# A two-layer hybrid decoder trunk: another order for its opening, and other rules for the list that orders its engines

## The chip, the cores and the metric

The kernel runs on one core of a Trainium2 chip, as one launch. The metric is the device time of that launch in microseconds (us). Before the change the median of three runs is 1262.36 us (1260.78 to 1263.79). The profile used here is of one further execution, which took 1262.23 us. Its profiled span, from the first to the last instruction, is 1260.5 us, so 1.73 us lie around the span.

## The reference

The program is a trunk of two layers over 256 tokens of width 1024, all in float32. Cut to what matters:

```python
c_act = silu(c)
for l in range(2):
    mod = c_act @ w_ada[l] + b_ada[l]                 # 1024 x 6144
    sh1, sc1, g1, sh2, sc2, g2 = split(mod, 6)
    h = rms_norm(x, norm1_g[l]) * (1 + sc1) + sh1
    proj = h @ w_in[l]                                # q k v iq ik iw z xbc dt ga gm
    q, k = rope(rms_norm(q)), rope(rms_norm(k)); iq, ik = rope(iq), rope(ik)
    # per block of 128 queries: score by iq, ik, iw; keep 64 keys; softmax attention on them
    o_attn = dsa_attention(q, k, v, iq, ik, iw, 64) @ w_attn_o[l]
    y = ssd_scan(silu(conv4(xbc)), softplus(dt), A)   # Mamba-2, then gate by silu(z), group norm
    mixed = (sigmoid(ga) * o_attn + sigmoid(gm) * (y @ w_ssm_o[l])) @ w_out[l]
    x = x + g1 * mixed
    h = rms_norm(x, norm2_g[l]) * (1 + sc2) + sh2
    val, gate = split(conv3(h @ w_up[l]), 2)
    x = x + g2 * ((silu(gate) * val) @ w_down[l])
```

## The kernel before

**The products.** Every weight matrix is streamed from HBM in units of up to 4 x 128 rows by 512 columns (1 MB). ACT rounds a unit to its high part `wh` (fp32r), DVE takes the low part `wl` = `st` - `wh`. The activations `h` are kept in the same two parts. A product is then three matmuls on PE: high by high, low weight by high, high weight by low activation. PE is busy with these almost throughout; the other engines prepare weights and evaluate what lies between products.

**The engines' order.** The program writes no order for ACT, DVE, POOL and the loads. Each operation is entered in a list with an estimate of its duration and its dependences. `plan_ahead` (line 122) plays the list forward: for each engine it takes the entered operation that could start first, where an operand that another engine or a transfer makes counts as there some time (`HOP`, line 59) after its end. `commit` issues all that the plan starts before PE's own clock `now` (line 190, where every row of the profile therefore says L190). PE's instructions are placed at once, in the order in which the code reaches them; `on_pe` (line 386) keeps the modelled time, and doubles the price of matmuls for a while after a long modelled wait. `pump` lets waiting tasks (attention, scan, transposes) put their matmuls in between as soon as the model says that their operands are there. So a number in `HOP` or in the price of a load changes no computation, but the order on all five engines, to the end of the program.

**The loads.** All weights come over SP's one DMA queue, at most six units ahead. Weight units have three buffers (`wst`), the modulation's units five (`wop`).

**The opening** (`run_open`, line 764). The first layer's norm needs shift and scale, 2048 columns of the modulation, which are 8 MB of `w_ada` in 8 units. They are done in four quarters `q` of 2 x 256 columns. In each quarter PE multiplies two units (`ada_products`: 16 matmuls of 32x128 from `st`, twice, into one bank), ACT copies the result (`adarow`), PE turns it, DVE makes `mod` and `amul`, and `norm_tile` makes two of the eight tiles of `h`, their high part on ACT and the low one on DVE. With two tiles of `h` the products with two of the eight row blocks of the first K columns, of the index queries IQ and of a narrow block (`misc`: index key, weights, dt) can be done. These are the `fills`: per quarter four, two for K with misc (9 matmuls each) and two for IQ (6 each). A fill is given to PE while the next modulation product is not there by the plan (line 839), or ahead of the next quarter's weights. The tables for the rotation (cosine, sine; `tables`, line 1003) are entered in quarter 1. `warm_up(n)` issues n 128x128 matmuls of ones whose result nobody reads; before the change there are 10 ahead of quarter 0 and 8 behind it.

In names: `st` is a loaded unit, `wh`, `wl` its parts, `w_4` the replicated silu(c), `rows` the small vectors before they are turned into `vec`, `bk` a PSUM bank, `p` the index scores, `top` the eight largest of them, `mx` the softmax maximum, `sp_p` the polynomial for softplus.

Of the kernel before, what the change touches and what calls it, by code (L numbers as in the profile page):

```python
# [46 lines left out]
def trunk(ctx, tc, x, c, positions, w_ada, b_ada, norm1_g, w_in, q_norm_g, k_norm_g, ssm_conv_w, ssm_conv_b,  # L47
# [6 lines left out]
    now = [0.0]  # L54
# [1 line left out]
    URGENT = 200  # L56


    HOP = dict(dve=33.0, act=33.0, pool=79.0, pe=54.0, dma=2500.0, dma_act=0.0, dma_pool=0.0)
    LAP = dict(dve=75.0, act=100.0, pool=30.0, dma=0.0, dma_act=0.0, dma_pool=0.0)  # L60
    CROWD = 0.18
    ORDER = ("dve", "act", "pool", "dma", "dma_act", "dma_pool")
    free_at = dict.fromkeys(ORDER, 0.0)
    waiting = {k: [] for k in ORDER}
# [57 lines left out]
    def plan_ahead():  # L122

        if not stale[0]:
            return
        stale[0] = False
        at = dict(free_at)
        todo = {k: list(v) for k, v in waiting.items() if v}
        crowd, slow = crowd_done[0], None
        for v in todo.values():  # L130
            for w in v:
                w.end = None
        while todo:
            best = None
            for key, ws in todo.items():
                first = None
                for w in ws[:1] if key == "dma" else ws:
                    t = w.least
                    for d in w.deps:
                        e = d.end  # L140
                        if e is None:
                            t = None
                            break
                        e += (HOP[key] if d.key[:3] != "dma" else HOP["dma"]) if d.key != key else -LAP["act"] if key == "act" else 0.0
                        if e > t:
                            t = e
                    if t is None:
                        continue
                    t = max(t, at[key])
                    if first is None or t < first[0]:  # L150
                        first = (t, w)
                        if t <= at[key]:
                            break
                if first and (best is None or first[0] < best[0]):
                    best = first + (key,)
            t, w, key = best
            w.start, w.end = t, t + w.ns
            if key == "pool":
                w.end = crowded(t, w.ns, crowd)
                slow = w  # L160
            elif w.heavy:
                crowd = w.end
                if slow and slow.end > t:
                    slow.end = crowded(t, slow.end - t, crowd)
                    at["pool"] = max(at["pool"], slow.end - LAP["pool"])
            at[key] = max(t + 0.4 * w.ns, w.end - LAP[key])
            todo[key].remove(w)
            if not todo[key]:
                del todo[key]
# [53 lines left out]
    def hold(tile):  # L223

        held.add(tile.tensor.name)
        return tile
# [130 lines left out]
    def enter_loads():  # L357
        while loads:
            out, src, issue = loads[0]
            t = out.tensor  # L360
            if t.name not in states and getattr(t, "tag", None):
                mine = rings.get(t.tag, ())
                if len(mine) >= (t.bufs or t.tag_meta.bufs) and not ripe(mine[0]):
                    return
            loads.pop(0)
            if not any(o.tensor.name == t.name for o, _, _ in loads):
                on_the_way.discard(t.name)
            give("dma", [out], [src], out.partition_size() * out.free_size() * 4 / (200.0 if now[0] < 1.0 else 300.0), issue, now[0] - 30000.0)

    def after(prev, cur):  # L370

# [14 lines left out]
    def on_pe(o, lhsT, rhs, issue, turn=False):  # L386
# [3 lines left out]
        at = now[0]  # L390
# [4 lines left out]
        ready = at  # L395
        for d in deps:
            if d.key != "pe":
                ready = max(ready, end_of(d, "pe"))
        if ready > at + 3000.0:
            slow_until[0] = ready + 3400.0  # L400
        at = ready
        w = Work("pe", 0.0, (), 0.0, issue)
# [361 lines left out]
    def run_open(ch):  # L764


        misc = hold(bank())
        tm = [[bank(pj) for _ in range(2)] for _ in range(2)]
        fills = []

# [30 lines left out]
        def fill():  # L801
            weigh(*fills.pop(0))

        def modulations():
            for q in range(4):
                ps = bank()
# [11 lines left out]
                        pass  # L818
                fence.clear()
                if q == 1:  # L820
                    for _ in tables():
                        pass
                    ch["start"]()
                while fills and fills[0][0] < q - 1:
                    fill()
                ahead(ch["w"][q], ch["w"][q] + 1)
                if q == 0:
                    ahead(ch["m"], ch["m"] + 1)
                    spare["bank"] = bank()
                    warm_up(8)  # L830
                fills.extend((q, w, j) for w in (1, 0) for j in range(2))

        ahead(0)
        for g in first:
            for _ in g:
                pass
        warm_up(10)
        for need in modulations():
            while fills and fill_need(*fills[0]).at() < need.at() and now[0] < need.at() - FILL:
                fill()  # L840
        ahead(ch["ada"][3][-1])
        done(crep)
        opening_done()
        while fills:
            fill()
        ch["evac"][0](tm[0])

    FILL = 300.0

    def opening_done():  # L850
        commit(1e12)
# [97 lines left out]

    def enter():  # L950
        sums = w_tile("xsum", [P, 2, 2], F32, 1)
        junk = spare["bank"] = bank(pj)
        for t, m4, xs_ in xin:
            A.activation(junk, xs_, AF.Square, accum_out=sums[:, t, m4:m4 + 1])
            ps = bank()
# [847 lines left out]
```

## Time and profile before

| | |
|---|---|
| median of 3 runs | 1262.36 us |
| profiled execution: its time, its span | 1262.23 us, 1260.5 us |
| PE, PEld, DVE, ACT, POOL busy | 97%, 90%, 76%, 60%, 33% |
| granted TensorE clock, mean | 0.989 |
| HBM | 243.89 MB read, 194 GB/s over the span |

The profile's page has busy shares, the span in 40 slices, the chain of waits that ended last, and groups of instructions. Since all instructions have one line, groups are told apart by the names of their tiles. A row of the timeline gives the start, the time until the last of the merged instructions ended, the engine, what it writes and reads, how many, and in brackets how long the engine stood idle before and what ended that. One float32 matmul appears as two records of 128x128, so 8 matmuls of ones are x16.

### The profile page before, as it was taken

The page shows a single profiled execution, that of the slowest core. Times are in us where ns is not written, and L with a number is a line of the kernel's source. Part 1 is how long each engine was busy: PE and PEld are TensorE (multiplying, and loading weights), DVE is VectorE, ACT ScalarE, POOL GpSimd, SP SyncE. Part 2 cuts the span into 40 slices and gives each one's busy share as a digit, 9 for nine tenths or more (in the row PEclk, how much of TensorE's full clock was granted, in tenths as well). Part 3 has the DMA queues.
Part 4 walks back from the last instruction along what each step waited for, and adds up shares of the span by engine and source line. Part 5 has one row for each costly group of instructions (what it writes and reads, how often), then busy time and mean ns, then how long its engine had stood idle before and what let it go on. Part 6 is the DMA issues. An engine that isn't in the chain of part 4 may idle for free.

```text
span 1260.5 us, 24567 instructions
## 1 busy us (share of the span) xinstructions
PE 1225.6 (97%) x9789; PEld 1140.5 (90%) x9789; DVE 956.3 (76%) x1477; ACT 762.2 (60%) x1362; POOL 414.3 (33%) x479
## 2 busy tenths in 40 slices
PE   7789999999999999999999999999999999999998
PEld 6577789999989999999997778999999999999998
DVE  4499977878786778889757997888777766678753
ACT  3356677774764357777436467877467544777742
POOL 2042533343262124564211443323304511335400
PEclk8889999999999999999989999999999999999999
DMA  9654644457456647876756455355764665566542
GB/s 300 231 182 144 209 146 171 163 193 255 159 203 215 234 156 239 276 248 229 247 180 201 148 195 193 126 170 172 240 204 153 215 236 166 181 209 202 195 162 73
DMA packets 158663, 246.53 MB, mean 196 GB/s; under 512 B 11868, under 2 KB 66870, under 8 KB 158549
## 3 DMA queue, kind: packets, MB, share of 16 engines
q1 hardware_dynamic: 157989, 244.77, 58.4%
q8 instruction: 77, 1.26, 0.4%
q14 instruction: 37, 0.30, 0.1%
q0 software_dynamic: 288, 0.19, 0.1%
q10 hardware_dynamic: 272, 0.00, 0.0%
HBM read 243.89 MB, written 1.05 MB: 194 GB/s over the span
## 4 chain that ended last, share of the span: by engine, by line
PE 79%; DVE 12%; ACT 4%; issue 3%; POOL 2%; DVEq 0%; POOLq 0%; ACTq 0%
PE bk L190 79%; DVE wl L190 4%; DVE w L190 1%; ACT wh L190 1%; DVE adacc L190 1%; DVE t L190 1%; DVE p L190 1%; POOL w L190 1%; ACT w L190 1%; ACT p L190 1%; DVE mx L190 1%; DVE ss L190 1%; DVE top L190 0%; POOL rows L190 0%; POOL rr L190 0%
## 5 line engine op out<-in xcount | busy, mean ns | idle before, releaser
L190 PE MATMUL bk<-h,wh 128*128 128x256 f32 x3488 | 646.8, 286 | 0.4 <-ACT h L190 0.4
L190 PEld LDWEIGHTS bk<-h,wh 128*128 128x128 f32 x3488 | 543.4, 192 | 12.1 <-issue 9.6
L190 DVE TENSOR_TENSOR wl<-st,wh 128x2048 fp32r<-128x2048 f32 (+1 forms) x200 | 435.0, 2179 | 146.4 <-ACT wh L190 146.0
L190 PE MATMUL bk<-h,wl 128*128 128x256 f32 x1744 | 492.0, 283 | 0.0
L190 ACT ACTIVATE wh<-st 128x2048 fp32r<-128x2048 f32 (+1 forms) x200 | 352.1, 1768 | 213.2 <-PE bk L190 176.7
L190 POOL TENSOR_TENSOR w<-w,w 128x254 f32<-128x254 f32 (+2 forms) x213 | 208.0, 992 | 416.1 <-DVE w L190 330.2
L190 PEld LDWEIGHTS bk<-h,wl 128*128 128x128 f32 x1744 | 334.1, 192 | 0.5
L190 PE MATMUL bk<-u,wh 128*128 128x256 f32 x1344 | 234.7, 279 | 0.0
L190 PEld LDWEIGHTS bk<-u,wh 128*128 128x128 f32 x1344 | 203.3, 188 | 1.6 <-issue 1.6
L190 PE MATMUL bk<-u,wl 128*128 128x256 f32 x672 | 186.1, 277 | 0.0
L190 PE MATMUL bk<-wh,h 128*128 128x512 f32 x448 | 150.4, 411 | 11.9 <-ACT wh L190 5.2
L190 ACT ACTIVATE w<-bk,vec 128x256 f32<-128x256 f32 (+2 forms) x272 | 122.2, 516 | 33.3 <-DVE w L190 19.6
L190 PEld LDWEIGHTS bk<-u,wl 128*128 128x128 f32 x672 | 126.2, 188 | 0.0
L190 DVE SCALAR_TENSOR_TENSOR adacc<-ad,chalf,adacc 128x512 f32<-128x512 f32 x140 | 121.6, 869 | 4.6 <-DMA ad<-in_w_ada_dram 4.0
L190 PEld LDWEIGHTS bk<-wh,h 128*128 128x128 f32 x448 | 83.8, 193 | 33.6 <-issue 8.0
L190 DVE SCALAR_TENSOR_TENSOR w<-bk,vec,w 128x255 f32<-128x255 f32 (+1 forms) x184 | 81.5, 475 | 16.4 <-ACT w L190 15.8
L190 PE MATMUL bk<-wl,h 128*128 128x512 f32 x224 | 90.4, 404 | 3.3 <-DVE wl L190 3.3
L190 POOL TENSOR_TENSOR u<-u,u 128x256 f32<-128x256 f32 (+1 forms) x56 | 67.3, 1219 | 57.4 <-ACT u L190 33.6
L190 POOL TENSOR_TENSOR rr<-ss,mhalf 128x16 f32<-128x16 f32 x8 | 26.0, 3254 | 98.3 <-DVE ss L190 98.3
L190 PEld LDWEIGHTS bk<-wl,h 128*128 128x128 f32 x224 | 43.4, 194 | 14.1 <-DVE wl L190 5.3
L190 ACT ACTIVATE w<-w 128x256 f32<-128x256 f32 x92 | 35.6, 412 | 30.3 <-POOL w L190 30.1
L190 ACT ACTIVATE u<-bk 128x128 f32<-128x128 f32 (+2 forms) x128 | 32.1, 325 | 30.7 <-PE bk L190 30.6
(194 smaller groups left out, 1178.5 us busy)
## 6 DMA issues: line engine op xcount, KB each, us to landing
st<-in_w_in_dram SPq DMA_DIRECT2D x80, 1024.0 KB, 5.1
st<-in_w_up_dram SPq DMA_DIRECT2D x88, 512.0 KB, 5.4
ad<-in_w_ada_dram SPq DMA_DIRECT2D x160, 256.0 KB, 5.4
st<-in_w_down_dram SPq DMA_DIRECT2D x20, 1024.0 KB, 5.3
st<-in_w_ssm_o_dram SPq DMA_DIRECT2D x16, 1024.0 KB, 5.3
st<-in_w_ada_dram SPq DMA_DIRECT2D x16, 512.0 KB, 10.2
st<-in_w_attn_o_dram SPq DMA_DIRECT2D x8, 1024.0 KB, 5.0
st<-in_w_out_dram SPq DMA_DIRECT2D x8, 1024.0 KB, 5.2
```

What stands on the lines that cost most here:

```text
L190: begun[n].issue()
```

## The change

It has these parts.

1. **The list.** An operand that a transfer brings counts as there 1300 ns after the end of the transfer (2500 before). The transfer itself is priced at 250 bytes per ns before PE's first matmul and 330 after (200 and 300), and starts at 2000 ns at the earliest. PE's price doubles after a modelled wait of 2000 ns (3000). And `PATIENCE`: an operation takes the place of an older one on an engine only if it could start earlier than that by more than 0.35 of its own duration; before, any lead was enough.
2. **The unread products.** They have a PSUM bank of their own from the start of `run_open` (held until the last modulation product), where they shared a bank with the unread result of ACT's squares. `keep_warm(need)` issues as many as fit, by the plan, before the operand that PE would wait for: int((wait - 300 ns) / 225 ns), if more than one. The two fixed lots (10 and 8) go.
3. **Which comes first.** A fill is still given only while the next modulation product is not there by the plan, but its margin `FILL` goes from 300 to 700 ns; with the transfers priced lower, the plan sees a modulation unit there earlier, and its product stands ahead of more fills.
4. **The tables** are entered in quarter 0, not in quarter 1.

```diff
-    HOP = dict(dve=33.0, act=33.0, pool=79.0, pe=54.0, dma=2500.0, dma_act=0.0, dma_pool=0.0)
+    HOP = dict(dve=33.0, act=33.0, pool=79.0, pe=54.0, dma=1300.0, dma_act=0.0, dma_pool=0.0)
+    PATIENCE = 0.35
...
-                    if first is None or t < first[0]:
+                    if first is None or t + PATIENCE * w.ns < first[0]:
                         first = (t, w)
...
-            give("dma", [out], [src], out.partition_size() * out.free_size() * 4 / (200.0 if now[0] < 1.0 else 300.0), issue, now[0] - 30000.0)
+            give("dma", [out], [src], out.partition_size() * out.free_size() * 4 / (250.0 if now[0] < 1.0 else 330.0), issue, max(2000.0, now[0] - 30000.0))
...
-        if ready > at + 3000.0:
+        if ready > at + 2000.0:
             slow_until[0] = ready + 3400.0
...
         misc = hold(bank())
+        spare["bank"] = hold(bank())
...
+        def keep_warm(need):
+
+            n = int((need.at() - now[0] - 300.0) / 225.0)
+            if n > 1:
+                warm_up(n)
...
                 if q == 1:
-                    for _ in tables():
-                        pass
                     ch["start"]()
...
                     ahead(ch["m"], ch["m"] + 1)
-                    spare["bank"] = bank()
-                    warm_up(8)
+                if q == 0:
+                    for _ in tables():
+                        pass
...
-        warm_up(10)
         for need in modulations():
             while fills and fill_need(*fills[0]).at() < need.at() and now[0] < need.at() - FILL:
+                keep_warm(fill_need(*fills[0]))
                 fill()
+            keep_warm(need)
         ahead(ch["ada"][3][-1])
-        done(crep)
+        done(crep, spare["bank"])
...
-    FILL = 300.0
+    FILL = 700.0
...
-        junk = spare["bank"] = bank(pj)
+        junk = bank(pj)
```

What this does to the order is seen at three places. The first is PE at the start of the opening, from behind the turning of the input to the first fill (`bk<-wh,h`); before:

```order
L190 MATMUL bk_137<-ones 128x128 x10
L190 MATMUL bk_143<-st_128,w_4_86 32x128 x16
L190 MATMUL bk_143<-st_129,w_4_86 32x128 x16
L190 MATMUL bk_289<-ident,rr_33_288 128x128 x2
L190 MATMUL bk_291<-ident,rows_81 128x128
L190 MATMUL bk_292<-ident,adarow_285 128x128
L190 MATMUL bk_303<-ones 128x128 x8
L190 MATMUL bk_126<-wh_134,h_294 128x512
```

The same place after the change:

```order
L191 MATMUL bk_124<-ones 128x128 x9
L191 MATMUL bk_144<-st_129,w_4_86 32x128 x16
L191 MATMUL bk_124<-ones 128x128 x11
L191 MATMUL bk_144<-st_130,w_4_86 32x128 x16
L191 MATMUL bk_291<-ident,rr_34_290 128x128 x2
L191 MATMUL bk_293<-ident,rows_81 128x128
L191 MATMUL bk_294<-ident,adarow_287 128x128
L191 MATMUL bk_124<-ones 128x128 x23
L191 MATMUL bk_127<-wh_135,h_296 128x512
```

The unread products stand now before each of the two modulation products, and 23 instead of 8 before the first fill. Two more lots stand behind quarters 0 and 1 (12 and 9).

The second place is PE at the end of quarter 2, where the last modulation unit is multiplied (`st_435` before, `st_481` after) and its result turned (`adarow`); the fills here are those of quarter 2 (K into bk_126 and bk_127 before, IQ into bk_124 and bk_125; one number higher after). Before:

```order
L190 MATMUL bk_125<-wh_564,h_558 128x512
L190 MATMUL bk_125<-wl_565,h_558 128x512
L190 MATMUL bk_125<-wh_564,h_559 128x512
L190 MATMUL bk_124<-wh_564,h_561 128x512
L190 MATMUL bk_124<-wl_565,h_561 128x512
L190 MATMUL bk_124<-wh_564,h_562 128x512
L190 MATMUL bk_125<-wh_564,h_561 128x512
L190 MATMUL bk_125<-wl_565,h_561 128x512
L190 MATMUL bk_125<-wh_564,h_562 128x512
L190 MATMUL bk_566<-st_435,w_4_86 32x128 x16
L190 MATMUL bk_680<-ident,adarow_679 128x128
L190 MATMUL bk_126<-wh_688,h_682 128x512
```

After:

```order
L191 MATMUL bk_123<-h_598,wh_303 128x256
L191 MATMUL bk_602<-st_481,w_4_86 32x128 x16
L191 MATMUL bk_125<-wh_600,h_594 128x512
L191 MATMUL bk_125<-wl_601,h_594 128x512
L191 MATMUL bk_125<-wh_600,h_595 128x512
L191 MATMUL bk_126<-wh_600,h_594 128x512
L191 MATMUL bk_126<-wl_601,h_594 128x512
L191 MATMUL bk_126<-wh_600,h_595 128x512
L191 MATMUL bk_719<-ident,adarow_705 128x128
L191 MATMUL bk_125<-wh_600,h_597 128x512
L191 MATMUL bk_125<-wl_601,h_597 128x512
L191 MATMUL bk_125<-wh_600,h_598 128x512
```

The last modulation product moved ahead of both IQ fills of quarter 2 (12 matmuls), of which now six lie between it and the turning of its result, and six behind that. In quarter 1 the second product and the turning moved in the same way.

The third place is DVE in the first layer's choice of 64 keys, where the two query blocks (128x128 and 128x256) go through eight rounds of eight largest (`MAX`) and their removal (`MATCH_REPLACE`). Before:

```order
L190 SCALAR_TENSOR_TENSOR p_173_1049<-p_198_1143,iws_829,p_173_1049 128x256
L190 MAX top_1168<-p_173_1049 128x8 x2
L190 MATCH_REPLACE p_173_1049<-top_1168,p_173_1049 128x128
L190 MATCH_REPLACE p_173_1049<-top_1168,p_173_1049 128x256
L190 MAX top_1168<-p_173_1049 128x8 x2
```

After:

```order
L191 SCALAR_TENSOR_TENSOR p_173_1095<-p_198_1191,iws_871,p_173_1095 128x256
L191 MAX top_1213<-p_173_1095 128x8
L191 MATCH_REPLACE p_173_1095<-top_1213,p_173_1095 128x128
L191 MAX top_1213<-p_173_1095 128x8
L191 MATCH_REPLACE p_173_1095<-top_1213,p_173_1095 128x256
```

Each removal stands now right behind the search whose result it reads, where the other block's work stood between them. Counted over the whole program, the DVE instructions that read what the one just before them wrote go from 62 to 180 (of 1445): 32 of the 118 more are removals, 29 are on `mx`, 29 on the convolutions' `w`, 15 on the softplus `sp`.

## Rows read from the trace of the kernel before

**Rows 1.** The page: its span, and the chain that ended last by engine.

```profile
span 1260.5 us, 24567 instructions
...
PE 79%; DVE 12%; ACT 4%; issue 3%; POOL 2%; DVEq 0%; POOLq 0%; ACTq 0%
```

**Rows 2.** Windows: stretch, length, busy us of the five engines, clock, DMA share, GB/s.

```profile
20.00:30.00 10.00, 8.86 (x60) 6.95 (x61) 5.08 (x21) 1.62 (x4) 0.00 (x0) 0.83 1.07 360
30.00:40.00 10.00, 4.91 (x45) 3.30 (x44) 6.15 (x25) 5.13 (x12) 0.00 (x0) 0.78 1.06 348
40.00:50.00 10.00, 8.96 (x91) 6.73 (x90) 2.41 (x8) 2.83 (x7) 2.85 (x12) 0.88 0.93 324
...
90.00:140.00 50.00, 48.66 (x250) 37.89 (x249) 48.27 (x117) 29.05 (x62) 15.69 (x14) 1.00 0.45 150
...
200.00:1260.00 1060.00, 1048.64 (x8561) 996.20 (x8560) 804.36 (x1121) 651.36 (x1113) 347.90 (x361) 1.00 0.59 195
```

**Rows 3.** Timeline of PE, last quarter of the opening: start, us, instructions, idle before.

```profile
58.13 1.08 PE L190 MATMUL bk<-st,w 128*32 128x128 f32 x32
...
62.00 0.50 PE L190 MATMUL bk<-wh,h 128*128 128x512 f32 x1 [2.06 <-ACT h L190]
63.06 0.79 PE L190 MATMUL bk<-wl,h 128*128 128x512 f32 x1 [0.56 <-DVE wl L190]
...
70.38 0.84 PE L190 MATMUL bk<-wh,h 128*128 128x512 f32 x3
```

**Rows 4.** Timeline of SP: the issue of the last modulation unit's loads.

```profile
38.41 1.87 SPq L190 DMA_DIRECT2D st<-in_w_ada_dram  x2
```

**Rows 5.** The page's DMA issues: count, KB each, median us to landing.

```profile
st<-in_w_ada_dram SPq DMA_DIRECT2D x16, 512.0 KB, 10.2
```

**Rows 6.** Timeline of PE, starts of the quarters, and the unread products.

```profile
10.41 3.56 PE L190 MATMUL bk<-ones 128*128 128x128 f32 x20 [2.05 <-ACT bk L190]
...
17.08 1.95 PE L190 MATMUL bk<-ones 128*128 128x128 f32 x16
...
21.64 0.62 PE L190 MATMUL bk<-wl,h 128*128 128x512 f32 x1 [1.03 <-DVE wl L190]
...
36.87 0.80 PE L190 MATMUL bk<-wh,h 128*128 128x512 f32 x1 [4.09 <-ACT wh L190]
```

**Rows 7.** Timeline of PE in quarter 1, at full clock.

```profile
42.82 0.50 PE L190 MATMUL bk<-wh,h 128*128 128x512 f32 x1
...
44.75 1.08 PE L190 MATMUL bk<-st,w 128*32 128x128 f32 x32
45.76 0.50 PE L190 MATMUL bk<-wh,h 128*128 128x512 f32 x1
...
47.28 0.27 PE L190 MATMUL bk<-ident,adarow 128*128 128x128 f32 x1
```

**Rows 8.** Timeline of DVE and of ACT (one row), the last quarter's chain.

```profile
59.98 0.23 DVE L190 TENSOR_TENSOR mod<-bk,vec 128x2 f32<-128x2 f32 x2 [8.10 <-PE bk L190]
...
60.93 0.87 DVE L190 SCALAR_TENSOR_TENSOR w<-xt,amul,w 128x256 f32<-128x256 f32 x2
61.72 1.28 DVE L190 TENSOR_TENSOR wl<-st,wh 128x512 fp32r<-128x512 f32 x2
...
61.44 0.91 ACT L190 ACTIVATE h<-w,mod 128x256 fp32r<-128x256 f32 x2 [0.33 <-DVE w L190]
```

**Rows 9.** Timeline of PE behind the opening: the wait for an IQ bank.

```profile
85.46 0.70 PE L190 MATMUL bk<-wh,h 128*128 128x512 f32 x2 [3.58 <-DVE sp_p L190]
```

**Rows 10.** Timeline of DVE: softplus steps one behind the other, then between other work.

```profile
93.10 0.22 DVE L190 TENSOR_TENSOR sp_p<-sp_p,sp_s 128x64 f32<-128x64 f32 x1
93.36 0.19 DVE L190 TENSOR_SCALAR sp_p<-sp_p 128x64 f32<-128x64 f32 x1
...
93.86 0.19 DVE L190 TENSOR_SCALAR sp_p<-sp_p 128x64 f32<-128x64 f32 x1
93.96 0.22 DVE L190 TENSOR_TENSOR t<-bk,sint 128x64 f32<-128x64 f32 x1
```

## The prediction

> **What bounds the kernel now.** I read the page's chain first: PE holds 79% of it and DVE 12% [rows 1]. Then the windows, to see where PE is not full. From 200 us to the end PE is busy for 1048.64 of 1060 us at a clock of 1.00, so 11.4 us are idle there in all; from 90 to 140 us it is busy for 48.66 of 50 while DVE is for 48.27; between 20 and 50 us it is busy for 8.86, 4.91 and 8.96 of 10 us at a clock of 0.78 to 0.88 [rows 2]. The program is bound by PE, and what can be taken is mostly in the opening. There the DMA share is about 1 until 50 us [rows 2], so loads bound the first half; not the second. The loads of the last modulation unit are issued from 38.41 on, the second at 40.28 at the latest [rows 4]; with the median of 10.2 us to landing [rows 5] they are there by 50.5. PE multiplies that unit at 58.13, after all fills of quarter 2, and only then starts the chain to the last two tiles of `h`: the fills of quarter 3 wait until 62.00 and 63.06 [rows 3]. That is 8 us lost by order alone.
>
> **The change part by part.** All is summed against the profiled execution (1262.23 us, against a median of 1262.36, so the same). Prices at full clock: a 9-matmul fill 44.75 - 42.82 = 1.93, a modulation unit 45.76 - 44.75 = 1.01, a 6-matmul fill 47.28 - 45.76 = 1.52 [rows 7], an unread product some 0.23 (8 in 1.95, the last outlasting its step) [rows 6]. The chain of a quarter, from T, when `adarow` is turned: `mod` 0.1 behind, then `amul`, the two `w` from T + 0.55 (before 0.95, with one `wl` of 0.6 between) to T + 1.4, the high `h` 0.5 behind the first `w`, the two low `h` as long as the `w`, to T + 2.35, and `wl` pieces at 0.61 each, of which the third lets the fill's second matmul go: T + 4.2 [rows 8].
>
> Start: loads are issued in the same order up to the 72nd row of SP, the first quarter's weights land when they did, and the low part that freed PE at 21.64 [rows 6] is no earlier. The bank of its own lets the unread products start at about 9 instead of 10.41 [rows 6], since they wait for a DVE copy and not for ACT. The 23 of them take 5.3 us and fit into the wait from some 16.2 to 21.6. So quarter 0 starts at 21.6 as before, but warm: the clock of 0.83 in 20 to 30 us [rows 2] becomes 1.
>
> Quarter 0 from 21.6: fill 23.5, unit 24.5, fill 26.5, fill 28.0, unit 29.0, turning of the small rows and of `adarow` 29.9, fill 31.4, 12 unread products 34.2. Loads bring a unit of 1 MB in 3 us (348 to 360 GB/s [rows 2]), so the two units of quarter 1 should be there at some 23.5 and 26.5. Its chain has one more copy (0.55 us for `vec`), so T = 30.4 and its third `wl` is at 34.6. Quarter 1 starts at 34.6, where before it started at 36.87 after 4.09 us idle [rows 6] and at half clock.
>
> Quarter 1 from 34.6: fill 36.5, unit 37.5, fill 39.5, unit 40.5, fill 42.0, turned 42.3, fill 43.8, 9 unread 45.9, unit of quarter 3 46.9. Its third `wl` (one piece is done early) is at 42.3 + 3.6 = 45.9, so PE does not wait. Quarter 2 from 46.9: fills 48.8 and 50.8, the last unit 51.8 (there by 50.5), fill 53.3, turned 53.6, fill 55.1. Quarter 3: its third `wl` at 53.6 + 4.2 = 57.8, PE having 2.5 us without work between 55.1 and then.
>
> Before, PE needed from 63.06 to 70.6 [rows 3] (the second of the three matmuls there is the first of the next slab) for the rest of quarter 3, 7.5 us, of which I estimate 3.4 at half clock after waits of 2.06 and 0.56 (a clock of 0.83 over 10 us, as behind the wait ahead of quarter 0 [rows 2], is 3.4 us at half). With 2.5 us of waiting again I take the same 7.5: the opening's products end at 57.8 + 7.5 = 65.3 instead of 70.6, a gain of 5.3. If the clock stays up, 1.7 more (half of 3.4): 7.0. If the first fill starts at 22.6, 1 less.
>
> Tables: some 25 small DVE operations, four sines and one ACT table load move from between 23 and 35 us, where they stood ahead of quarter 1's chain, to 11 to 16 us, where DVE and ACT wait for the first units. Their cover is that wait; without it they would cost their 2 to 3 us at the first quarter, which still had the loads of 20 us ahead. I take nothing. The other bank that is held leaves two rotating banks for the opening's small results instead of three; each is read within 0.6 us of being written, so nothing, up to 0.5 us a quarter.
>
> Behind the opening, PE stands 3.58 us at 85.46 [rows 9]: its next slab needs the bank that DVE reads for the rotation of IQ. DVE's work from the K result to that read is the same set of operations, and starts when K's products end, so it moves up with them and the wait stays. From 90 us on PE is bound, and the gain of 5.3 goes through to the end.
>
> The list's numbers: they move some 290 rows of PE and many of DVE, ACT and POOL, all the way to the end, and SP's loads by a few places from the 73rd row on. No matmul comes or goes but 46 unread ones in waits. What this does to the 11.4 us of idle PE behind 200 us cannot be read off: bounds are -4 (a third of it goes) and, from the DVE pairs, +10 (below); I take 0, nearest to the 1% that PE idles there.
>
> The 118 more DVE instructions right behind the one whose result they read: a dependent step starts 93.36 - 93.10 = 0.26 after the one ahead, an independent one 93.96 - 93.86 = 0.10 [rows 10]. So up to 0.16, say 0.13 each, 15 us of DVE. DVE is busy for 804 of 1060 us behind 200 [rows 2], so most of it is free; from 90 to 140, with 48.27 of 50, it is not. [...]
>
> **Rivals.**
> *DVE becomes the bound (slower).* Place: the two dense stretches (90 to 140 us, and its like in the second layer) and the attention between. There are 26 pairs in each of the two (16 removals, about 7 of `sp`, 3 of `ss`) and 29 of `mx`, in all 81; at 0.13 that is 10.5 us. If PE waits for all of it, 1262.23 - 5.3 + 10.5 = 1267.4. It decides from 60 pairs on PE's path on (5.3 + 2.5 = 7.8 us). For it: DVE's 48.27 of 50. Against: the plan sees these pairs and places PE's work later accordingly, and PE waited only 1.34 us in that stretch.
> *The gain is given back (no change).* The opening is 5 us shorter, but the wait of 3.58 us grows, or transfers counted as there 1.2 us earlier than before let ACT and DVE stand in front of one that has not landed. At 3 to 5 us of new waits in 1190 us: 1260 to 1262. For it: small moves in every stage; against: nothing in the opening's sum depends on them.
> *The clock stays up and the list saves too (more).* 7.0 and 3 of the 11.4 us: 1252.2.
> *The order does not move.* Excluded by the order itself, which has the last unit ahead of 12 matmuls.
>
> **How the numbers follow.** Forecast: opening 5.3 us shorter, the rest as it was: 1262.23 - 5.3 = 1256.9, from 1254 to 1259.5 by the clock, the start and 1.5 us of small waits; chance 0.57. More: 0.13. Given back, within 0.2% (2.5 us either way, about what a measurement of this kernel tells from no change): 0.18. Slower: 0.12. So faster 0.70, same 0.18, slower 0.12. The range of 8 in 10 goes from 1251.5 (the third rival) to 1263 (the second with its worst end and a little of the first).
>
> **What would show it.** The last unit's product (`st,w`) at about 51 instead of 58.13; quarter 3's second matmul near 57.8; the first matmul of the next slab near 65.3; a clock of 1 between 20 and 50 us; the 3.58 us still there, some 5 us earlier. Behind 90 us the same idle PE as before within 2 us. I am wrong if the slab behind the opening starts later than 68, if PE's idle time behind 90 us grows by more than 3 us with DVE named as releaser, or if a unit is multiplied late with a DMA named as the releaser.

## The result, and the profile after

The changed kernel is slower: 1279.39 us (1278.67 to 1282.12), against 1262.9 for the kernel before beside it; ratio 1.0137, 95% interval [1.0117, 1.0157]. The forecast was 1256.9. The opening did what was forecast; 22 us are lost behind it.

The page after, span and chain, answers [rows 1]:

```profile
span 1277.3 us, 24697 instructions
...
PE 60%; DVE 20%; ACT 7%; POOL 5%; issue 5%; DMA 2%; SPq 0%; DVEq 0%; POOLq 0%; ACTq 0%
```

PE held 79% of the chain before and 60% now; DVE 20% instead of 12%. More of what the end depends on now runs through engines other than PE.

The windows after, columns as in [rows 2]; the last runs from the first slab behind the opening to the end:

```profile
20.00:30.00 10.00, 10.00 (x95) 8.95 (x94) 5.30 (x11) 3.56 (x8) 0.00 (x0) 1.00 1.06 359
30.00:40.00 10.00, 9.79 (x112) 7.89 (x111) 5.03 (x12) 3.26 (x7) 0.00 (x0) 1.00 1.02 336
40.00:50.00 10.00, 10.00 (x109) 8.30 (x109) 5.08 (x11) 3.33 (x7) 4.97 (x12) 1.00 0.90 311
...
90.00:140.00 50.00, 47.22 (x236) 35.88 (x235) 47.48 (x97) 26.70 (x52) 18.63 (x10) 1.00 0.47 158
...
65.25:1277.30 1212.05, 1179.89 (x9350) 1101.69 (x9348) 943.78 (x1373) 737.33 (x1300) 424.85 (x416) 1.00 0.56 188
```

The stretch of before that answers to the last row:

```profile
70.38:1260.50 1190.12, 1172.71 (x9350) 1099.32 (x9348) 923.92 (x1375) 735.09 (x1302) 403.29 (x416) 1.00 0.58 192
```

The opening runs at a clock of 1.00, where [rows 2] have 0.78 to 0.88. Behind it the same 9350 PE instructions take 1212.05 instead of 1190.12 us, at the same clock of 1.00: 21.9 more. PE's idle time grows from 17.4 to 32.2 us, and PE's recorded busy time by 7.2 us, for the same instructions. At full clock the record of a 128x512 matmul is 0.39 to 0.5 us long, while nine in a row take 1.93 us, 0.21 each; so a wait shorter than the difference shows as busy and not as idle. DVE is busy for 19.9 us more with two instructions fewer.

PE's timeline after, columns as in [rows 3]:

```profile
19.11 5.30 PE L191 MATMUL bk<-ones 128*128 128x128 f32 x46
24.16 0.48 PE L191 MATMUL bk<-wh,h 128*128 128x512 f32 x1
...
36.07 0.48 PE L191 MATMUL bk<-wh,h 128*128 128x512 f32 x1
...
52.27 1.08 PE L191 MATMUL bk<-st,w 128*32 128x128 f32 x32
...
57.57 0.51 PE L191 MATMUL bk<-wh,h 128*128 128x512 f32 x1 [1.10 <-ACT wh L191]
59.38 0.49 PE L191 MATMUL bk<-wl,h 128*128 128x512 f32 x1 [1.30 <-DVE wl L191]
...
65.25 0.84 PE L191 MATMUL bk<-wh,h 128*128 128x512 f32 x3
...
81.11 0.70 PE L191 MATMUL bk<-wh,h 128*128 128x512 f32 x2 [3.79 <-DVE sp_p L191]
```

The last modulation unit is multiplied at 52.27 (before 58.13) and the next slab begins with the second matmul of the row at 65.25, at 65.48 (before 70.60): 5.1 us earlier, where 5.3 were forecast. The wait for the IQ bank is there still, 3.79 for 3.58 [rows 9].

What PE waited for after: us in total, times, the longest.

```profile
PE bk L191 <- DVE wl L191: 5.7, 8, 1.3
PE bk L191 <- DVE t L191: 4.4, 4, 1.7
PE bk L191 <- DVE sp_p L191: 3.8, 1, 3.8
PE bk L191 <- ACT adarow L191: 3.6, 3, 1.6
PE bk L191 <- DVE u L191: 3.2, 5, 1.2
PE bk L191 <- DVE adacc L191: 2.8, 3, 1.5
```

No single wait carries the loss (that for `sp_p` was there before): it is many, none over 1.7 us, most of them for the ends of DVE's chains (`t` the rotation, `u` attention, `adacc` the second layer's modulation, `wl` the weights).

What DVE waited for, two lines of after, then the two of before:

```profile
DVE adacc L191 <- DMA ad<-in_w_ada_dram: 22.5, 17, 3.7
DVE u L191 <- ACT u L191: 22.3, 27, 2.0
```

```profile
DVE u L190 <- ACT u L190: 4.2, 5, 1.4
DVE adacc L190 <- DMA ad<-in_w_ada_dram: 4.0, 1, 4.0
```

So there are two suspects: the loads' numbers (DVE stands 18.5 us longer in front of transfers that have not landed) and the patience (it stands 18 us longer for ACT's `u`); the pairs, DVE instructions right behind the one whose result they read, are a third, and part of the second. These rows are no price by themselves: DVE's longest wait in total, that of `wl` for ACT's `wh`, fell at the same time from 146.0 to 65.9 us.

DVE in the first choice of keys shows the pairs' price. Before, one round of both blocks:

```profile
118.72 0.61 DVE L190 MAX8 top<-p 128x8 f32<-128x256 f32 x2
119.24 0.07 DVE L190 MATCH_VALUE_LOAD p<-top,p 128x8 f32 x1
119.30 0.41 DVE L190 MATCH_REPLACE8 p<-top,p 128x256 f32<-128x256 f32 x1
119.63 0.08 DVE L190 MATCH_VALUE_LOAD p<-top,p 128x8 f32 x1
119.70 0.27 DVE L190 MATCH_REPLACE8 p<-top,p 128x128 f32<-128x128 f32 x1
119.89 0.61 DVE L190 MAX8 top<-p 128x8 f32<-128x256 f32 x2
```

After:

```profile
116.03 0.28 DVE L191 MAX8 top<-p 128x8 f32<-128x128 f32 x1
116.34 0.09 DVE L191 MATCH_VALUE_LOAD p<-top,p 128x8 f32 x1
116.42 0.28 DVE L191 MATCH_REPLACE8 p<-top,p 128x128 f32<-128x128 f32 x1
116.61 0.42 DVE L191 MAX8 top<-p 128x8 f32<-128x256 f32 x1
117.07 0.09 DVE L191 MATCH_VALUE_LOAD p<-top,p 128x8 f32 x1
117.14 0.41 DVE L191 MATCH_REPLACE8 p<-top,p 128x256 f32<-128x256 f32 x1
117.47 0.28 DVE L191 MAX8 top<-p 128x8 f32<-128x128 f32 x1
```

A round goes from 1.17 us (118.72 to 119.89) to 1.44 (116.03 to 117.47): 0.135 for each of its two pairs. The gap stands where the prediction's rows have it: the value load (the first record of a removal) starts 0.03 us behind the end of the search it reads, whereas before, with the other block's search in front of it, it started 0.09 us ahead of that search's end.

### The profile page after: what moved, and what is told of

It is laid out like the page before. It is cut to its first block, busy times and chain, and to the rows that moved or that the text cites. A ratio compares the mean times of both kernels' runs of the same rounds, so it can differ in the third digit from the quotient of the medians.

```text
span 1277.3 us, 24697 instructions
## 1 busy us (share of the span) xinstructions
PE 1237.7 (97%) x9881; PEld 1150.0 (90%) x9881; DVE 977.4 (77%) x1477; ACT 766.0 (60%) x1362; POOL 438.0 (34%) x479
## 4 chain that ended last, share of the span: by engine, by line
PE 60%; DVE 20%; ACT 7%; POOL 5%; issue 5%; DMA 2%; SPq 0%; DVEq 0%; POOLq 0%; ACTq 0%
PE bk L191 60%; DVE wl L191 8%; POOL w L191 4%; DVE w L191 4%; ACT w L191 3%; ACT wh L191 3%; DVE adacc L191 2%; DMA ad<-in_w_ada_dram 2%; DVE t L191 2%; DVE p L191 1%; DVE u L191 1%; DVE top L191 1%; ACT u L191 1%; POOL u L191 0%; DVE mx L191 0%
## 5 line engine op out<-in xcount | busy, mean ns | idle before, releaser
L191 PEld LDWEIGHTS bk<-h,wh 128*128 128x128 f32 x3488 | 542.5, 191 | 12.2 <-issue 10.1
L191 DVE TENSOR_TENSOR wl<-st,wh 128x2048 fp32r<-128x2048 f32 (+1 forms) x200 | 430.9, 2167 | 69.4 <-ACT wh L191 65.9
L191 POOL TENSOR_TENSOR u<-u,u 128x256 f32<-128x256 f32 (+1 forms) x56 | 77.4, 1402 | 56.6 <-DVE u L191 30.2
L191 POOL TENSOR_TENSOR rr<-ss,mhalf 128x16 f32<-128x16 f32 x8 | 29.7, 3706 | 81.0 <-DVE ss L191 81.0
```

What stands on the lines that cost most here:

```text
L191: begun[n].issue()
```

## The experiments

To place losses I compare when the same weight matmul (by its count in the program) starts; a minus is earlier than before. From the traces, in us; the first column is the time in the kernel before:

```
before   change  opening  switch  short   short  pairs   change,
                 only     back    holds   small  in top  no pairs
  70.60   -5.12   -2.91   -8.56    3.77    4.29   0.71    -5.46
 121.32   -4.31   -2.95   -7.65    4.34    4.83   0.70    -8.01
 151.07   -2.99   -2.91   -7.64    4.45    8.23   4.41   -12.64
 309.07   -0.69   -2.94   -7.65    9.20    7.87   3.95    -6.97
 335.27    3.38   -2.94   -7.65    9.20    7.87   3.95    -5.75
 396.43    0.79   -2.95   -7.65    9.10    5.81   3.95    -7.17
 443.24    1.56   -2.95   -7.65    9.10   20.91   3.95    -7.17
 620.29    5.36   -3.63   -7.66   12.55   25.61   3.24    -0.09
 755.87    5.25   -3.94   -7.64   10.72   29.44   4.41     1.97
 968.77   12.11   -3.95   -7.65   12.70   29.42   4.41    -0.40
1147.78   10.68   -3.95   -7.66   19.03   36.95   4.40    -0.40
1255.62   16.76   -3.95   -7.66   20.77   36.95   4.40     3.98
```

The first row differs by some 0.5 to 0.7 us between profiles whose code is the same up to there (the kernel before and `pairs_in_top`; `switch_back` and `pairs_in_top_2`); what a run gains or loses behind it is the rest of the column. The count is of weight matmuls only, so attention work that is put off shows as a lead for a while (last column).

**Opening alone** (`only_opening`): all list numbers back.

```diff
-    HOP = dict(dve=33.0, act=33.0, pool=79.0, pe=54.0, dma=1300.0, dma_act=0.0, dma_pool=0.0)
+    HOP = dict(dve=33.0, act=33.0, pool=79.0, pe=54.0, dma=2500.0, dma_act=0.0, dma_pool=0.0)
...
-    PATIENCE = 0.35
+    PATIENCE = 0.0
...
-            give("dma", [out], [src], out.partition_size() * out.free_size() * 4 / (250.0 if now[0] < 1.0 else 330.0), issue, max(2000.0, now[0] - 30000.0))
+            give("dma", [out], [src], out.partition_size() * out.free_size() * 4 / (200.0 if now[0] < 1.0 else 300.0), issue, now[0] - 30000.0)
...
-        if ready > at + 2000.0:
+        if ready > at + 3000.0:
```

> The changed kernel with all the list's numbers of before (transfers counted as there 2500 ns later at 200 and 300 B/ns, threshold 3000, no patience); the unread products, FILL and the tables' place stay changed. In the changed kernel the slab behind the opening starts 5.1 us earlier (65.48 against 70.60), and the end comes 16.8 us later: 21.9 us are lost behind it. Theory 'patience' (engines held for older work lose them) and theory 'loads' (transfers counted as there too early) both have the opening's gain go through: about 1257.5, slab behind the opening near 65.5, idle PE behind it near the 13.8 us of before. Theory 'any order' (whatever shifts the lists costs as much, since the numbers of before happen to fit) has 1265 to 1279. Patience or loads: less than 1260.

1258.28 us, a ratio of 0.9975 to the kernel before beside it [0.9964, 0.9987]. The lead stays flat for 500 us and does not shrink to the end: the opening's gain goes through, as the first two theories have it. It is a smaller gain than the changed kernel's: the slab behind the opening starts 2.9 us earlier and not 5.1, since the loads' numbers, which are back here, have a part in the opening too (`loads_only`, below). "Any order" has nothing to answer here, since PE's times behind the opening hardly move against each other.

**Without patience** (`patience_0`): `PATIENCE = 0.0`, all else as changed.

> The changed kernel with PATIENCE 0, the loads' numbers as changed. DVE instructions right behind the one whose result they read: 78 (180 with patience, 62 before). Patience: the 21.9 us go, 1257 to 1260. Loads: nothing goes, 1276 to 1281, and DVE still waits some 20 us for ad. Each by half: about 1268. Any order: 1265 to 1280, without a pattern.

1266.47, 1.0042 [1.0027, 1.0057]. By the ratios 12 of the 17 us go. In the trace the slab behind the opening starts 7.0 us earlier than before and the end comes 4.7 later, so 11.8 us are still lost behind the opening (21.9 in the changed kernel). DVE's wait for `ad` is still there:

```profile
DVE adacc L191 <- DMA ad<-in_w_ada_dram: 16.5, 15, 3.0
```

**Loads' numbers back** (`loads_back`): `dma=2500.0`, 200 and 300 B/ns, no least start; patience kept.

> The changed kernel with the loads' numbers of before (2500 ns, 200 and 300 B/ns, no least start), PATIENCE 0.35 kept. Loads: 1257 to 1260, and DVE's wait for ad falls from 22.5 us to about the 4 us of before. Patience: 1276 to 1281 with the wait for ad gone all the same. Each by half: about 1268. Any order: 1265 to 1280.

1278.34, 1.0137 [1.0120, 1.0154]: in total nothing goes, though DVE's wait for `ad` falls to 5.3 us. In the trace the slab behind the opening starts 2.6 us earlier than before and the end comes 16.4 later: 19.0 us are lost behind the opening instead of 21.9. While there is patience, the loads' numbers cost some 3 us there, and the opening gives as much.

**Patience alone** (`only_patience`): the kernel before with the two lines of patience.

> The kernel before with PATIENCE 0.35 and nothing else. Patience: 1262.4 + 21.9, about 1284, idle PE behind the opening 28 us instead of 13.8. Loads: 1261 to 1264. Each by half: about 1273. Any order: 1266 to 1284.

1285.24, 1.0191 [1.0176, 1.0206]: 24 us, as that theory said (1284). Patience alone is enough for a loss of this size.

**Short holds, and holds without pairs.** Patience makes an engine stand for an older operation (long holds) and puts a reader right behind the writer (pairs). `short_holds` caps a hold at 80 ns:

```diff
-                    if first is None or t < first[0]:
+                    if first is None or t + min(0.35 * w.ns, 80.0) < first[0]:
```

> The kernel before, where an operation takes the place of an older one only if it could start earlier by more than 0.35 of its duration or 80 ns, whichever is less. An instruction that reads what the one ahead of it on its engine wrote is put 75 ns later by the plan on DVE, so these short holds make the same pairs (182 on DVE, 175 with patience 0.35), but no engine stands for an operation that comes later than 80 ns. Patience alone cost 1285.2 - 1261.3 = 23.9 us. Theory 'pairs' (the dependent neighbours cost it): about 1280 to 1286. Theory 'long holds' (engines stand for operations that are hundreds of ns away, and the next ones are late): 1261 to 1266. Half each: 1273.

1281.44, 1.0155 [1.0138, 1.0173]. `holds_no_pairs` keeps the long holds and drops the others:

```diff
+                    if first is None or (t < first[0] if first[0] <= at[key] + LAP[key] + 1.0 else t + 0.35 * w.ns < first[0]):
```

> The kernel before with patience 0.35, but without a hold for an older operation that comes no later than its own engine's lap (75 ns on DVE, 100 on ACT): 60 dependent neighbours on DVE (62 before), the long holds stay. Pairs: 1260 to 1264. Long holds: 1280 to 1286. Half each: 1273.

1270.93, 1.0074 [1.0059, 1.0089]. Short holds alone cost 19.5 us and long ones 9; together 24, so the two don't add. Neither theory has all of it; the short holds, which make the pairs, have most.

**Patience on DVE alone** (`patience_dve`): `0.35 * w.ns if key == "dve" else 0.0`.

> The kernel before with patience 0.35 on DVE alone; ACT, POOL and the loads are planned as before. With patience everywhere PE's idle time behind the opening has DVE as releaser for most of the increase (t 5.95, wl 4.77, adacc 3.88 us). If it is DVE that is held too long or slowed by pairs: 1278 to 1286, nearly all of the 23.9. If ACT's and POOL's holds make DVE late (DVE waits 22 us longer for w of ACT and 20 for u of ACT): 1261 to 1268.

1281.85, 1.0157 [1.0140, 1.0174]: 20 of the 24 us; it is DVE's patience.

**Which operations stand back** (`short_small`, `short_big`). Short holds only where the one that stands back is at most 1000 ns long, and only where it is longer.

> As the run with short holds (80 ns at most, 1281.4 us), but an operation of over 1000 ns (a weight's low part on DVE above all) takes its place as before: only small ones stand back for an older one. 153 dependent neighbours on DVE (182 with all short holds, 62 before). Theory 'pairs': the loss goes with their number, 19.5 x 91 / 120 = 14.8, about 1277. Theory 'displaced weights' (the long low part of a weight, which PE waits for, stands behind chains of small steps): 1261 to 1266.

1292.80, 1.0256 [1.0224, 1.0287]: 31 us, more than all short holds.

> The other half: only operations of over 1000 ns stand back, if the older one comes at most 80 ns later. 67 dependent neighbours on DVE. Pairs: 1262 to 1264. Displaced weights: 1275 to 1282.

1267.29, 1.0040 [1.0025, 1.0055]. Displaced weights are out: where the weights keep their place the loss is greatest. But a loss in proportion to the number of pairs is out too (1277 expected). Most of the excess is at one place, between 396 and 443 us of before, where 15 us are lost. The same 46.8 us of the kernel before and what they take in `short_small`, columns as in [rows 2]:

```profile
396.43:443.24 46.81, 46.81 (x411) 46.48 (x410) 34.45 (x41) 21.14 (x24) 6.58 (x9) 1.00 0.70 237
```

```profile
402.27:464.15 61.88, 54.50 (x415) 52.80 (x414) 37.80 (x49) 22.22 (x27) 9.93 (x11) 0.89 0.62 208
```

PE stands for 7.4 us, several times in a row for `u` and `xdt`, the activations of its products, and a clock of 0.89 over 61.88 us is 6.8 us of work at full clock: the two are nearly all of the 15. In PE's timeline of `short_small`:

```profile
409.31 0.38 PE L190 MATMUL bk<-u,wh 128*128 128x256 f32 x1 [1.74 <-ACT u L190]
411.80 0.39 PE L190 MATMUL bk<-u,wh 128*128 128x256 f32 x1 [2.11 <-DVE u L190]
413.92 0.58 PE L190 MATMUL bk<-xdt,wh 128*128 128x256 f32 x1 [0.36 <-DVE xdt L190]
```

(Its profile is of the slowest of its four runs, 1299.18.) That the weights, which kept their place here, went in front of that chain's steps is a reading of mine that no run tests.

Over the whole run, too, the clock is much of the difference between the two: `short_small`'s mean granted clock is 0.977 over a span of 1297.5 us, that of `short_holds` 0.988 over 1281.3. By my estimate the low clock takes 29.8 us of full-clock work in the first and 15.4 in the second, 14 of the 16 us that lie between the two profiled executions. (Some of the low clock falls on idle time, so this is an upper estimate.)

**The loads alone, and two shaken lists.** `loads_only` is the kernel before with the loads' new numbers; `list_shaken` and `list_shaken_2` have 2300 and 2700 ns for 2500.

> The kernel before with the loads' new numbers alone (1300 ns, 250 and 330 B/ns, least start 2000). Without patience and with the new opening they lost 11.8 us behind the opening (-7.04 us at its end, +4.7 at the end). Theory 'loads': 1268 to 1276, DVE waits 12 to 20 us for ad (4 before). If they only lose together with the new opening: 1260 to 1264.

1261.0, 0.9992 [0.9978, 1.0005]: no loss in total, though DVE waits for `ad` as in the changed kernel:

```profile
DVE adacc L190 <- DMA ad<-in_w_ada_dram: 19.5, 15, 3.4
```

Its profile is of the fastest of its ten runs (1256.76). There the last modulation unit is multiplied at 52.29 us (58.13 before), the slab behind the opening starts 6.2 us earlier and the end comes 5.5 earlier: the loads' numbers alone bring the opening's gain, without the unread products, and in this execution 0.8 us are lost behind it. Why the median shows only 0.8 us of that gain stays open, as no slower run of it was profiled.

> A control: the kernel before with a transfer counted as there after 2300 ns in place of 2500, a change that no theory gives a price; the order moves on all engines, 70 dependent neighbours on DVE. Theory 'any order': 1268 to 1280 like the others. Pairs and loads: 1259 to 1266.

1265.12, 1.0029 [1.0019, 1.0039].

> Second control: the kernel before with a transfer counted as there after 2700 ns in place of 2500, 65 dependent neighbours. The first control cost 0.29%. As a measure of what any new order costs: 1260 to 1267; theory 'any order' as the cause of the 17 us: 1270 or more.

1267.56, 1.0040 [1.0025, 1.0055]. In these two controls a new order without any reason costs 0.3 and 0.4% (3.3 and 6.0 us by the medians). That is the floor under every comparison above where the order moves: the 17 us are well over it, the 5 us of `short_big` are within it.

**Pairs out of the changed kernel** (`change_no_pairs`): the rule of `holds_no_pairs` in the changed kernel.

> The changed kernel (1278 to 1279), but patience makes no hold for an older operation that comes within its own engine's lap, so that 54 dependent neighbours stand on DVE instead of 180; all else as changed. Theory 'pairs', as a cost of the order that goes with them or of their own time: the whole of what short holds cost alone (19.5) should be most of what is won back: 1262 to 1268, the patience_0 run being 1266.5. Theory 'long holds' or 'loads': 1275 to 1280.

1265.65, 1.0028 [1.0016, 1.0040]: 13.7 of the 17 us are won back with all the rest as changed. In the trace 9.4 us are still lost behind the opening, for 21.9. The rule takes out every hold within a lap, not only those that make pairs.

**Pairs without any rule** (`pairs_in_top`): in the kernel before the search and the removal are entered as one operation.

```diff
-                    V.max(top[:, t, :], sc[:, cs])
-                    V.match_replace(sc[:, cs], top[:, t, :], sc[:, cs], DEAD)
+                    def both_steps(t=t, cs=cs):
+                        nc.vector.max(top[:, t, :], sc[:, cs])
+                        nc.vector.match_replace(sc[:, cs], top[:, t, :], sc[:, cs], DEAD)
+                    n_ = sc[:, cs].free_size()
+                    give("dve", [top[:, t, :], sc[:, cs]], [sc[:, cs]], 2 * (155.0 + 1.06 * n_) - LAP["dve"], both_steps)
```

> The kernel before with its own rules, but each search of the eight largest and the removal that reads it are entered as one operation: 94 dependent neighbours on DVE, 32 more, all of them in the two choices of keys. In the changed kernel's trace a round of two blocks takes 1.45 us (116.03 to 117.47) against 1.18 before (113.71 to 114.89), so 0.135 a pair. If the pairs' own time is what is lost: 32 x 0.135 = 4.3 us more DVE time in the two dense stretches, 1264 to 1266.5. If it is the order that goes with short holds (older chains finished first), and not the pairs' time: 1259 to 1263.

1267.36, 1.0047 [1.0033, 1.0062]: 5.8 us for 32 pairs (4.3 priced). By the medians alone that is within the floor, but its trace shows the place: its column above steps up by 3.7 us at the first choice; then nothing is lost until the second (it drifts back by 1.5 up to 698 us), where it steps up by 1.5; behind that it is flat. Net of the opening that is 3.7 us in this profile. PE's waits at the two places in that run, then in the kernel before:

```profile
134.25 0.65 PE L190 MATMUL bk<-ident,t 128*128 128x128 f32 x4 [2.89 <-DVE t L190]
...
754.80 0.63 PE L190 MATMUL bk<-ident,t 128*128 128x128 f32 x4 [2.26 <-DVE sums L190]
```

```profile
131.43 0.66 PE L190 MATMUL bk<-ident,t 128*128 128x128 f32 x4 [1.34 <-DVE t L190]
...
750.39 0.63 PE L190 MATMUL bk<-ident,t 128*128 128x128 f32 x4 [0.77 <-DVE sums L190]
```

Each of these waits for DVE grows by 1.5 us, which is the whole step at the second choice. At the first choice it is less than half of the step: behind the wait of 2.89 us the granted clock falls to the lower of its two levels (1.2 instead of 2.4 GHz) for a while, and matmuls that start 0.22 us apart in the kernel before start 0.43 apart; behind the wait of 1.34 us it stays. The windows behind the wait, of `pairs_in_top` and of the kernel before, clock in the third column from the end:

```profile
135.00:140.00 5.00, 5.00 (x19) 4.00 (x18) 4.93 (x10) 1.00 (x6) 0.00 (x0) 0.66 0.02 3
```

```profile
135.00:140.00 5.00, 5.00 (x28) 3.67 (x27) 4.95 (x12) 2.69 (x4) 0.37 (x1) 1.00 0.57 182
```

At 0.66 five us give 1.7 us less of work. So the 16 pairs of the first choice, 2.2 us of DVE, cost some 2 us of waits and 1.7 us of clock.

The same 32 pairs on another base, that of the next run:

> The kernel of switch_back (1254.7) with the same 32 pairs forced as in pairs_in_top. There the first slab behind the first choice of keys lost 3.7 us and that behind the second 1.5 us, nothing elsewhere, 5.2 in all by the trace and 5.8 by the medians. If these pairs cost their own time wherever they stand in a dense stretch: 1254.7 + 5.2 = 1259.9, from 1258.5 to 1261.5. If it was a new order's luck: 1253 to 1257.

1259.47, 0.9982 [0.9969, 0.9995], 4.8 us over that base, 5.2 expected. In the trace the wait at the first choice is 2.89 us again, where the base has 1.34, and the column steps up there by 3.7 us again. That the pairs' own time is a cost is shown, and that a longer wait can cost clock besides.

**The opening with its numbers, the rest as before** (`switch_back`): patience 0, and at the end of the opening

```diff
+        HOP["dma"] = 2500.0
```

with 300 B/ns, the old least start and the threshold of 3000 from there on.

> The changed kernel with patience 0, and with the loads' numbers and the threshold of before from the end of the opening on; the opening itself is that of the run without patience, whose first slab behind it starts at 63.56, 7.04 us earlier than before. Theory 'loads' (the new numbers lose behind the opening): all 7 us get through, 1254 to 1255.5, DVE waits for ad as before (about 4 us), idle PE behind the opening about 13.8 us. Theory 'any order': 1258 to 1268, since the order behind the opening is entered from another state.

1254.67, 0.9942 [0.9927, 0.9957]. The column is flat from 121 us to the end. **This beats both kernels.** `patience_0` (1266.47) has the same opening and differs only behind it, by the loads' numbers and the threshold: 11.8 us by the medians; in the traces 11.8 us are lost behind the opening there and 0.9 here. So without patience these numbers cost some 11 us behind the new opening, about twice the larger control. `later_switch` keeps the changed numbers, without pairs, up to 210 us:

> The changed kernel without pairs (1265.7), with patience, the loads' numbers and the threshold set back to those of before at the first weight matrix chunk that the plan enters after 210 us. Without pairs that kernel stood 10 to 12 us ahead of the kernel before at 250 to 290 us, by the count of weight matmuls, and lost it all later. If the lead is real, 1250 to 1253; if it is only other PE work put off (it had shrunk to 5.7 us by 338 us), 1254 to 1258, no better than switch_back.

1253.03, 0.9939 [0.9919, 0.9960]: no better that can be told. In its trace the lead is 13.8 us at 151 us, 8.2 at 309 and 10.1 at the end: a part of it was other work put off.

## Why the prediction was wrong

*The opening: right.* Forecast and measured: quarter 0 at 21.6, 24.16; quarter 1 at 34.6, 36.07; last unit some 51, 52.27; second matmul of quarter 3 57.8, 59.38; next slab 65.3, 65.48. The steps are 1.2 to 2.6 us late, and the rest of quarter 3 takes 6.1 instead of 7.5, since the clock stays up: two errors that cancel, so that 5.1 for 5.3 is in part luck. The first comes from the unread products. I let them end when the weights were ready; the list's estimate of the wait was longer than the wait, and the 46 records from 19.11 hold PE until 24.16 without a gap. The prediction's "if the clock stays up, 1.7 more" was the term that held.

*Tables, bank: not contradicted* by the opening's sum, and neither was tried alone. The operands of the first fill were there at 21.54 us, forecast 21.6, though ACT and DVE still had steps of the tables (`cost`) between 18.65 and 19.9 us. Two slips move no forecast: 57.8 - 55.1 is 2.7 and not 2.5, and the third rival's sum is 1252.2, not the range's 1251.5.

*The wait of 3.58 stays: right* (3.79).

*"From 90 us on PE is bound, and the gain of 5.3 goes through to the end": right of a gain in the opening* (`only_opening`, `switch_back`), wrong of the changed kernel. Behind 90 us PE's idle time grows from 13.8 to 28.1 us, most of it with DVE named: the prediction's own sign of being wrong (more than 3 us).

*The 118 pairs: here it failed.* The price of one was right, 0.13 forecast and 0.135 measured in the choice of keys. The Trainium skill (VectorE: DVE Perf Modes, "The DRAIN you can't avoid") says that a next operation that is not held starts before the pipe has emptied. The round of the kernel before agrees, its value load starting 0.09 us ahead of the search's end. What failed is the sentence after the price, "DVE is busy for 804 of 1060 us behind 200 [rows 2], so most of it is free". By `change_no_pairs` the 126 pairs fewer, with the holds that make them, give back 13.7 us; by `short_holds` 120 more cost 19.5: 0.11 to 0.16 us of the whole program's time for each, as if DVE were the bound everywhere. These two rules move the order as well; with little else moved (`pairs_in_top`) it is 3.7 us net for 32 by the trace, 0.12 each. PE waits for the ends of chains, and a chain's length counts the pairs whether DVE is otherwise busy or not. So the rival "DVE becomes the bound" named a cause, its chance of 0.12 was too small and its 1267.4 too low, and its place was too narrow: from 90 to 140 us PE's idle time grows only from 1.34 to 2.78 us, and in the table the changed kernel loses most outside the dense stretches (4 us from 309 to 335, 7 from 756 to 969, 6 behind 1148). Which of these losses are the pairs' the runs don't separate.

*Patience itself: not priced.* The prediction read of it only the pairs it makes. Its long holds cost 9 us alone (`holds_no_pairs`), some of which may be any new order's price.

*"The list's numbers: I take 0" between -4 and +10: wrong too.* The two controls say +3 to +6 for a shift without a reason, and the loads' numbers cost more than that behind the new opening. In the traces the loss behind the opening is 21.9 us as changed, 11.8 without patience, 19.0 with the loads' numbers back and about none with both back (-1.0 in `only_opening`, 0.9 in `switch_back`). So both cost, and they overlap: patience 10 us on top of the new numbers and 20 without them, the numbers 3 us on top of patience and 11 without it. With the old opening and no patience they cost 0.8 us (`loads_only`, one execution), so this price belongs to the order that they meet and not to the numbers alone.

*Open:* why small operations that stand back bring so much longer waits and lower clock than all of them together (31 us and 19.5); why patience and the loads' numbers overlap. The 9 us that the changed kernel without pairs lies over the forecast (1265.7 - 1256.9) arise behind 210 us: `later_switch`, which differs only from there on, lies at 1253.0. How much of them is long holds and how much loads no run separates.

## What to carry to other kernels

An engine's share of busy time doesn't say that a longer chain on it is free; look for what the bounding engine waits at the chain's end, and whether its clock falls behind that wait. In a scheduler, price a reader right behind its writer at what the trace shows (here 0.135 us more than with another step between), and let a younger operation go between them. Change the numbers of a planner only for the stage that gains by them (1254.67 us here for 1266.47), and measure a shift without meaning first: what that costs is the least that can be told.

## What was not expected of the hardware

Unread products can be too long a cover: the 23 from 19.11 to 24.16 held PE while the first `wl` was done. In the changed kernel one row each of ACT's timeline and of DVE's:

```profile
20.57 0.91 ACT L191 ACTIVATE h<-w,mod 128x256 fp32r<-128x256 f32 x2
```

```profile
20.85 0.69 DVE L191 TENSOR_TENSOR wl<-st,wh 128x512 fp32r<-128x512 f32 x1
```

At 21.54 the first fill had all that its first two matmuls read (`h` at 21.48, `wl` at 21.54).

The granted clock stood at 1.00 (2.4 GHz) through these products and through the two waits of 1.10 and 1.30 us, and fell in the opening's wake only behind the 3.79 us without work:

```profile
50.00:60.00 10.00, 7.60 (x63) 5.61 (x62) 4.63 (x12) 5.21 (x9) 0.00 (x0) 1.00 0.35 124
60.00:66.00 6.00, 6.00 (x31) 5.04 (x30) 4.43 (x7) 5.42 (x8) 0.70 (x1) 1.00 0.82 293
80.00:90.00 10.00, 8.88 (x40) 7.31 (x41) 9.62 (x28) 2.85 (x13) 4.04 (x6) 0.83 0.27 99
```
